# Moving the sample tile's gathered experts from the dense stretch into the head of a one-core encoder step

## The chip, the core and the metric

The kernel runs on one core of a Trainium2 chip. The core has TensorE (PE in the profile), VectorE (DVE), ScalarE (ACT), GpSimd (POOL) and SyncE (SP), each with its own instruction queue that is worked off in order, and 16 DMA engines that all queues share. The metric is the device time of one execution in microseconds; the time before is the median of three runs.

## The reference

The step is one layer of a streaming encoder on 1024 prompt frames and 64 sample frames. After the mixers (windowed attention and retention) every frame `h` goes through PEER: 8 heads pick 16 experts each out of 16384 by product keys, so 128 experts for a frame, and

```python
s1, i1 = lax.top_k(s[:, :, 0], PEER_TOPK)
s2, i2 = lax.top_k(s[:, :, 1], PEER_TOPK)
...
eidx = jnp.take_along_axis(cand_i, sel, axis=-1)
g = jax.nn.softmax(top_s, axis=-1)
act = jax.nn.gelu(jnp.einsum('tpkd,td->tpk', u_tab[eidx], xb, preferred_element_type=jnp.float32))
w = (g * act).astype(xb.dtype)
return jnp.einsum('tpk,tpkd->td', w, v_tab[eidx])
```

followed by `layer_norm(ALPHA * h + peer, ln2_g, ln2_b)`. Rows of `u_tab` and `v_tab` have 1024 float32 values.

## The kernel before

**Tiles.** There are nine tiles of frames: eight of the prompt (0 to 7, 128 frames each) and `TS` = 8, the 64 sample frames. Tiles 0 to 4 (`DENSE`) are computed against all 16384 experts on PE, with a table `G` of gate weights in DRAM. Tiles 8, 5, 6 and 7 (`GT`, in this order) are *gathered*: for each of a frame's 128 experts, rows of `u` and `v` are fetched. A *slot* is one such fetch for 128 partitions: an indirect DMA on POOL's queue (line 239) brings 128 rows of 8 KB (u and v side by side, 1.05 MB) into a buffer `uv`. The sample tile has two experts of its 64 frames side by side in a slot, so 64 slots; the other three have 128 each: 448 in all.

**Stages.** `head` does the groups `[8, 0, 1]`, `[2, 3]`, `[4, 5]`, `[6, 7]` in turn: `qkv`, `mixer`, `posts`, `keys`. After a group's keys its tiles are appended to `bg`, generators of `route` that find the expert indices on DVE. `mid` builds `G` for tiles 2, 3 and 4 with one-hot products. The *dense stretch* runs 128 passes of `u_mm` (48 matmuls into `pA` each) with the `v_mm` products into `y` between them.

**G by scatter.** For tiles 0 and 1 (`SCAT`) the table `G` is filled by 256 scatters on POOL's queue (line 373), 128 for each tile; from the 17th on a tile's scatter adds to what is there, and each waits on POOL until the tile's one before has landed. `scatter` is called in `bulk`, in the keys and in `mid`.

**The order by hand.** The program's order is written by a planner that adds up estimated times (`Est`). In the head, `bulk` keeps a credit `cr` of DVE time (0.92 of PE's estimated time less what DVE was given, at most 7) and spends it on steps of `bg`. For POOL it keeps `pq`, the time to which POOL is booked: a scatter adds `SCC` = 1.6 and a gather `GTC` = 1.1, and a scatter is placed only while `pq` is no more than 5 ahead:

```python
if t in sc and links[t] < 128 and (n < rush or (due[t] <= now() and ctl["pq"] <= now() + 5.0)):
```

A slot may be placed once the planner's clock has reached `avail`, which is the booked time plus a `slack`:

```python
ctl["avail"][k] = max(est.t["dma"] + 2.0, max(ctl["pq"], now()) + ctl["slack"])
```

While it is built, the kernel prints how many scatters of tiles 0 and 1 stand in the program at each group's end: 0 and 0, 43 and 41, 98 and 97, 128 and 128.

**A slot before.** All 448 slots are in the dense stretch (`ctl["uvp"]` is `None` until then). `slot` multiplies and sums u with `h` on DVE (`uv<-uv,ph`, with a read of the accumulator), `settle` does the gelu and the gate on ACT (`gav`), `accum` adds the weighted v row to `pacc` in PSUM on DVE. At most `LEAD` = 3 gathers are ahead, in `NB` = 4 buffers. After a tile's last slot, `finish` and `norm_out` do the last norm, whose power is on POOL (`mvf`); `norm_out` lets four steps go by between it and the DVE instruction that reads it.

Of the kernel before, what the change touches and what calls it, by code (L numbers as in the profile page):

```python
# [9 lines left out]
F32 = mybir.dt.float32  # L10
# [4 lines left out]
AF = mybir.ActivationFunctionType  # L15
OP = mybir.AluOpType
AX = mybir.AxisListType

D = 1024
# [5 lines left out]
TS = NTP  # L25
# [12 lines left out]
NB, LEAD = 4, 3  # L38
# [15 lines left out]
SL = (30.0, 5, 5.0)  # L54
FA, FB = 8, 5
NVS, NWB = 6, 6
KW = 256 + NM + 1
KWS = 128 + NS + NM + 1

# [76 lines left out]
def hymba_peer_step(ctx, tc, a, o):  # L136
    nc0 = tc.nc
    est = Est()
# [7 lines left out]
    nc = NC  # L146
    ctx.enter_context(tc.manual_schedule())
    gat = ctx.enter_context(tc.tile_pool(name="gat", bufs=1))
    rx = ExitStack()
    rt = rx.enter_context(tc.tile_pool(name="rt", bufs=1, side="right"))  # L150
# [7 lines left out]
    sfac = gat.tile([128, 1], F32, name="sfac")  # L158
# [6 lines left out]
    spill = {}  # L165
# [43 lines left out]
    ready = {t: False for t in range(NTP + 1)}  # L209
    GT = [t for g in GROUPS for t in g if t not in DENSE]  # L210
    slots = [(t, j) for t in GT for j in range(64 if t == TS else 128)]
    ctl = dict(most=3, k=0, issued=0, done=-1, avail=[0.0] * len(slots), fin=[], uvp=None, ln2=None, gps=None, lead=LEAD, slack=9.0, cr=0.0, pe0=0.0, dve0=0.0, ph=0, pq=0.0)
    tl, rows_uv = {}, {}

    def open_tile(t):
        d = spill[t]
        h1 = gat.tile([128, D], F32, name="gh1")
        g = gat.tile([128, 128], F32, name="gg", bufs=2)
        idx = gat.tile([128, 128], I32, name="gi", bufs=2)
        if t == TS:  # L220
            for i, (lo, hi) in enumerate(((0, NS), (NS, 128))):
                nc.sync.dma_start(h1[lo:hi], d["h1"])
                nc.sync.dma_start(g[lo:hi, 0:64], d["g"][:, i * 64:(i + 1) * 64])
                nc.sync.dma_start(idx[lo:hi, 0:64], d["idx"][:, i * 64:(i + 1) * 64])
        else:
            nc.sync.dma_start(idx, d["idx"])
            nc.sync.dma_start(h1, d["h1"])
            nc.sync.dma_start(g, d["g"])
        av = gat.tile([128, 128], F32, name="gav", bufs=2)
        tl[t] = dict(h1=h1, g=g, idx=idx, av=av, left=64 if t == TS else 128)  # L230

    def issue():
        k = ctl["issued"]
# [37 lines left out]
    def finish(t, d):  # L271
        r, q = d["acc"], 128
        ln2, late = ctl["ln2"], t == TS
        if ln2 is None or t == TS:
            x = ctl["uvp"].tile([128, 2 * D], F32, name="lnx", tag="uv")
            ln2 = [x[:, 0:D], x[:, D:2 * D]]
            nc.sync.dma_start(ln2[0], rows_bcast(a["ln2_g"], D))
            if t == TS:
                q = NS
                nc.sync.dma_start(ln2[1][0:NS], r[NS:128])  # L280
                yield
                yield
                yield
                yield
                nc.vector.tensor_tensor(r[0:NS], r[0:NS], ln2[1][0:NS], op=OP.add)
            nc.sync.dma_start(ln2[1], rows_bcast(a["ln2_b"], D))
        yield from norm_out(gat, t, r, q, ln2)

    def norm_out(pool, t, r, q, ln2, st=None):
        wide = st is not None  # L290
        if not wide:
            st = pool.tile([128, 2, 6], F32, name="stf", bufs=2)
            for i, x in enumerate(halves(r)):
                nc.vector.bn_stats(st[:q, i], x[:q])
        mv = pool.tile([128, 3], F32, name="mvf", bufs=2)
        nc.vector.bn_aggr(mv[:q, 0:2], st[:q])
        nc.vector.tensor_scalar(mv[:q, 1:2], mv[:q, 1:2], EPS, None, op0=OP.add)
        nc.gpsimd.tensor_tensor(mv[:q, 2:3], mv[:q, 1:2], epsc[:q, 0:1], op=OP.pow)
        if wide:
            nc.gpsimd.tensor_tensor(mv[:q, 0:1], mv[:q, 0:1], mv[:q, 2:3], op=OP.mult)  # L300
            nc.gpsimd.tensor_scalar(mv[:q, 0:1], mv[:q, 0:1], -1.0, None, op0=OP.mult)
            yield
            nc.scalar.activation(r[:q], r[:q], AF.Identity, bias=mv[:q, 0:1], scale=mv[:q, 2:3])
            yield
            nc.gpsimd.tensor_tensor(r[:q], r[:q], ln2[0][:q], op=OP.mult)
            yield
            eng = nc.gpsimd if DENSE.index(t) in PAD else nc.vector
            eng.tensor_tensor(r[:q], r[:q], ln2[1][:q], op=OP.add)
            nc.sync.dma_start(o["y_p"][t * 128:(t + 1) * 128, :], r)
            return  # L310
        for _ in range(4):
            yield
        nc.vector.scalar_tensor_tensor(r[:q], r[:q], mv[:q, 0:1], ln2[0][:q], op0=OP.subtract, op1=OP.mult)
        yield
        nc.vector.scalar_tensor_tensor(r[:q], r[:q], mv[:q, 2:3], ln2[1][:q], op0=OP.mult, op1=OP.add)
        if t == TS:
            nc.sync.dma_start(o["y_s"], r[:q])
        else:
            nc.sync.dma_start(o["y_p"][t * 128:(t + 1) * 128, :], r)
# [5 lines left out]
    def prefetch():  # L325
        if ctl["uvp"] is None:
            return
        while (ctl["issued"] < len(slots) and ctl["issued"] < ctl["k"] + ctl["lead"]
               and ready[slots[ctl["issued"]][0]]):
            issue()  # L330

# [29 lines left out]
    def now():  # L361
        return max(est.t["pe"], est.t["dve"])

    links, due = {t: 0 for t in SCAT}, {t: 0.0 for t in SCAT}
    sc = {}

# [14 lines left out]
        return n  # L381

    zq = [(t, i) for t in SCAT for i in range(8)]
    zeros = rt.tile([128, 512], F32, name="zeros")
    nc.vector.memset(zeros, 0.0)

    def clear():
        t, i = zq.pop(0)
        nc.sync.dma_start(spill[t]["G"].rearrange("(p a n) o -> p a (n o)", p=128, n=512)[:, i * 4:(i + 1) * 4],
                          zeros[:, None, :].to_broadcast([128, 4, 512]))  # L390

    def pump(most, room=1.0):
        prefetch()
# [17 lines left out]
    def log(what):  # L411
        print("phase end", what, {k: round(v) for k, v in est.t.items()}, ctl["k"], len(bg), list(links.values()))
# [13 lines left out]
    def bulk(n):  # L426
        pe, dve = est.t["pe"], est.t["dve"]
        ctl["cr"] = min(CRMAX, ctl["cr"] + CRATE * (pe - ctl["pe0"]) - (dve - ctl["dve0"]))
        ctl["n"] = ctl.get("n", 0) + 1
        if zq and ctl["n"] % ZP == 0:  # L430
            clear()
        while scatter():
            pass
        for i in range(n):
            if ctl["cr"] <= 0.0:
                break
            d0 = est.t["dve"]
            step_bg()
            ctl["cr"] -= est.t["dve"] - d0
        ctl["pe0"], ctl["dve0"] = est.t["pe"], est.t["dve"]  # L440

    def head(hx):
# [2 lines left out]
        wrk = hx.enter_context(tc.tile_pool(name="wrk", bufs=2))  # L445
        sml = hx.enter_context(tc.tile_pool(name="sml", bufs=2))
        late = hx.enter_context(tc.tile_pool(name="late", bufs=4))
        pps = [hx.enter_context(tc.tile_pool(name=f"pps{i}", bufs=1, space=bass.MemoryType.PSUM)) for i in range(2)]

        def bank(tag):  # L450
# [549 lines left out]
        for gi, tiles in enumerate(GROUPS):  # L1000
# [33 lines left out]
            for t in sorted(tiles, key=lambda t: t not in DENSE):  # L1034
                bg.append(route(t, VI[t], NS if t == TS else 128))
                kind.append(t in DENSE)
            log("group")

    def route(t, VI, q):
        V, I = VI[:, 0], VI[:, 1].bitcast(U32)  # L1040
# [565 lines left out]
```

## Time and profile before

| | |
|---|---|
| median of 3 runs | 3328.54 us (3322.7 to 3331.77) |
| the profiled execution | 3355.53 us, span 3353.8 us |
| PE busy | 2904.7 us, 87% |
| DVE busy | 2265.5 us, 68% |
| POOL busy | 1781.7 us, 53% |
| ACT busy | 1115.8 us, 33% |
| granted PE clock, mean | 0.934 |
| DMA | 813.19 MB, 242 GB/s over the span |

Times in the rows are microseconds from the span's start, or nanoseconds where a row says mean ns. A row that names a releaser says what ended the engine's idle time. A busy share is an average over its stretch. The head takes the first 1030 us or so, the dense stretch begins at about 1260 us.

### The profile page before, as it was taken

To read this page: it belongs to the slowest core of one execution; us is meant where nothing else is said; L and a number is where in the kernel's file an instruction comes from. 1 tells how busy PE (TensorE), PEld (TensorE's weight loads), DVE (VectorE), ACT (ScalarE), POOL (GpSimd) and SP (SyncE) were. 2 spreads that over 40 slices of the span, in tenths; PEclk is the share of its full clock that TensorE was granted. 3 is DMA by queue.
4 is the path that set the end of the run, shared out by engine and by line. 5 is a ranking of instruction groups with operands and counts; after the bars stand their busy time and mean duration, and the time that the engine had idled before them with its cause. 6 is when DMAs were issued, how large, how long until landed. Compare 5 with 4: busy or idle time off the path is not lost.

```text
span 3353.8 us, 43782 instructions
## 1 busy us (share of the span) xinstructions
PE 2904.7 (87%) x15212; PEld 2495.5 (74%) x15212; DVE 2265.5 (68%) x5539; ACT 1115.8 (33%) x2599; POOL 1781.7 (53%) x1326
## 2 busy tenths in 40 slices
PE   4999889898996568888899988989899899989996
PEld 3777767677775557777788877878788788878895
DVE  1436976738639964776777777777778677877424
ACT  2332232332424663333333333333333333333221
POOL 0000155676663555665666666666666566666544
PEclk8999899899897789999999999999999999999998
DMA  6435235436432468898999989899989899999531
GB/s 178 145 112 213 82 84 145 95 62 167 97 79 79 114 181 325 326 346 304 349 355 354 350 336 340 321 347 341 355 323 361 318 349 349 351 367 340 199 98 63
DMA packets 296470, 813.19 MB, mean 242 GB/s; under 512 B 58296, under 2 KB 164520, under 8 KB 229176
## 3 DMA queue, kind: packets, MB, share of 16 engines
q0 software_dynamic: 97792, 469.94, 39.3%
q1 hardware_dynamic: 198024, 340.12, 29.9%
q8 instruction: 120, 1.97, 0.2%
q14 instruction: 102, 0.84, 0.1%
q10 hardware_dynamic: 432, 0.33, 0.0%
HBM read 753.04 MB, written 56.97 MB: 242 GB/s over the span
## 4 chain that ended last, share of the span: by engine, by line
PE 39%; DVE 22%; DMA 13%; issue 11%; POOL 10%; ACT 3%; SPq 1%; POOLq 0%; DVEq 0%; ACTq 0%
PE pA L108 13%; PE y L108 10%; DMA uv<-uv,gi 9%; PE pv L108 4%; PE pq L108 4%; DVE VI L108 4%; PE pa L108 3%; POOL uv L239 3%; POOL vl L108 3%; DVE pacc L108 3%; DVE ge L108 2%; DVE ob L108 2%; POOL ul L108 2%; POOL wl L108 2%; DVE oh L108 2%
## 5 line engine op out<-in xcount | busy, mean ns | idle before, releaser
L239 POOL DMA_INDIRECT uv<-uv,gi x448 | 432.1, 965 | 619.8 <-DVE pacc L108 561.2
L373 POOL DMA_INDIRECT G<-sg,si x256 | 382.3, 1493 | 620.2 <-DVE si L108 383.3
L108 DVE SCALAR_TENSOR_TENSOR uv<-uv,ph 128x1024 f32<-128x1024 f32 x448 | 544.1, 1215 | 238.1 <-DMA uv<-uv,gi 234.0
L108 PE MATMUL y<-vh,wh 128*128 128x512 f32 x1280 | 530.7, 415 | 185.1 <-DVE Y L108 182.9
L108 DVE SCALAR_TENSOR_TENSOR pacc<-uv,gav,pacc 128x1024 f32<-128x1024 f32 x448 | 575.6, 1285 | 2.2 <-ACT pacc L108 2.1
L108 PE MATMUL y<-vl,wh 128*128 128x512 f32 x1280 | 521.7, 408 | 2.0 <-POOL vl L108 2.0
L108 PE MATMUL y<-vh,wl 128*128 128x512 f32 x1280 | 520.8, 407 | 0.0
L108 PEld LDWEIGHTS y<-vh,wh 128*128 128x128 f32 x1280 | 250.8, 196 | 270.8 <-DVE Y L108 173.6
L108 DVE TENSOR_TENSOR Y<-y,Y 128x512 f32<-128x512 f32 x420 | 280.6, 685 | 178.8 <-PE y L108 175.1
L108 POOL TENSOR_TENSOR vl<-vr,vh 128x512 fp32r<-128x512 f32 x256 | 327.9, 1294 | 100.5 <-ACT vh L108 49.9
L108 PEld LDWEIGHTS pA<-xhi,uh 128*128 128x128 f32 x2048 | 331.5, 199 | 37.1 <-DVE ge L108 24.1
L108 PE MATMUL pA<-xhi,uh 128*128 128x320 f32 x2048 | 338.6, 320 | 23.3 <-DVE ge L108 23.3
L108 ACT ACTIVATE gav<-gav 128x1 f32<-128x1 f32 x448 | 88.7, 198 | 706.5 <-DVE uv L108 693.7
L108 PE MATMUL pA<-xlo,uh 128*128 128x320 f32 x2048 | 321.7, 309 | 0.0
L108 PE MATMUL pA<-xhi,ul 128*128 128x320 f32 x2048 | 321.2, 309 | 0.0
L108 POOL TENSOR_TENSOR ul<-ur,uh 128x1024 fp32r<-128x1024 f32 x128 | 309.6, 2418 | 4.8 <-ACT uh L108 2.5
L108 PEld LDWEIGHTS pA<-xlo,uh 128*128 128x128 f32 x2048 | 306.5, 188 | 0.0
L108 PEld LDWEIGHTS pA<-xhi,ul 128*128 128x128 f32 x2048 | 305.6, 187 | 0.0
L108 PEld LDWEIGHTS y<-vh,wl 128*128 128x128 f32 x1280 | 252.9, 198 | 57.0
L108 PEld LDWEIGHTS y<-vl,wh 128*128 128x128 f32 x1280 | 252.5, 197 | 48.9 <-POOL vl L108 2.9
L108 ACT ACTIVATE pA<-pA 128x640 f32<-128x640 f32 x128 | 88.0, 688 | 511.9 <-PE pA L108 505.9
L108 DVE TENSOR_TENSOR ge<-pA,gt 128x640 f32<-128x640 f32 x128 | 105.2, 822 | 212.0 <-ACT pA L108 145.3
(287 smaller groups left out, 4385.4 us busy)
## 6 DMA issues: line engine op xcount, KB each, us to landing
ur<-ut SPq DMA_DIRECT2D x128, 512.0 KB
vr<-vt SPq DMA_DIRECT2D x256, 256.0 KB
gt<-G SPq DMA_DIRECT2D x320, 128.0 KB
w<-w_r SPq DMA_DIRECT2D x32, 1024.0 KB
G<-gs SPq DMA_DIRECT2D x24, 1024.0 KB
G<-zeros SPq DMA_DIRECT2D x16, 1024.0 KB
w<-w_out SPq DMA_DIRECT2D x16, 1024.0 KB
w<-w_pq SPq DMA_DIRECT2D x16, 1024.0 KB
```

The costliest lines, as they stand in the source:

```text
L108: return f(*a, **k)
L239: nc0.gpsimd.indirect_dma_start(out=R, out_offset=None, in_=a["uv"], in_offset=bass.IndirectOffsetOnAxis(ap=tl[t]["idx"][:, j:j + 1], axis=0))
L373: nc0.gpsimd.indirect_dma_start(out=spill[t]["G"], out_offset=bass.IndirectOffsetOnAxis(ap=idx[:, j:j + 1], axis=0), in_=g[:, j:j + 1], in ...
```

## The change

The 64 slots of the sample tile are placed in the head, as credit allows, once that tile is routed; slots that find no place there go on in the dense stretch. In `bulk`, each step of `bg` is followed by a `half` if credit is left: either the u product of the next slot (`udot_head`) or the v product of an earlier one (`vacc_head`). Both are on DVE in SBUF; the gelu is five ACT instructions on one column in place of the two of `settle`. Up to `LEADH` = 4 gathers are ahead, in `NBH` = 5 buffers of a pool of the head, and `slack` is 12. To make room, the tile of zeros with which `G` is cleared is halved. At the head's end the slots in flight are worked off. `finish` and `norm_out` let fewer steps go by, for all gathered tiles.

```diff
-    ctl = dict(most=3, ..., lead=LEAD, slack=9.0, ...)
+    ctl = dict(most=3, ..., lead=LEADH, head=True, turn=0, slack=12.0, ...)
...
+        gh = None
+        if ctl["head"]:
+            gh = rt.tile([128, 64], F32, name="ggh")
+            nc.scalar.activation(gh, g[:, 0:64], AF.Copy, scale=0.5)
...
-                yield
-                yield
                 nc.vector.tensor_tensor(r[0:NS], r[0:NS], ln2[1][0:NS], op=OP.add)
...
-        for _ in range(4):
-            yield
+        yield
         nc.vector.scalar_tensor_tensor(r[:q], r[:q], mv[:q, 0:1], ln2[0][:q], op0=OP.subtract, op1=OP.mult)
...
-        while (ctl["issued"] < len(slots) and ctl["issued"] < ctl["k"] + ctl["lead"]
+        while (ctl["issued"] < (64 if ctl["head"] else len(slots)) and ctl["issued"] < ctl["k"] + ctl["lead"]
...
+    def udot_head(k):
+        t, j = slots[k]
+        d = tl[t]
+        R = rows_uv[k]
+        av = d["av"][:, j:j + 1]
+        if j == 0:
+            d["acc"] = gat.tile([128, D], F32, name="gacc")
+            nc.scalar.activation(d["acc"], d["h1"], AF.Copy, scale=sfac)
+        nc.vector.scalar_tensor_tensor(R[:, 0:D], R[:, 0:D], 1.0, d["h1"], op0=OP.mult, op1=OP.mult, accum_out=av)
+        u = rt.tile([128, 3], F32, name="gu", bufs=4)
+        nc.scalar.activation(u[:, 0:1], av, AF.Square, scale=math.sqrt(0.044715))
+        nc.scalar.activation(u[:, 1:2], u[:, 0:1], AF.Identity, scale=av, bias=av)
+        nc.scalar.activation(u[:, 2:3], av, AF.Copy, scale=d["gh"][:, j:j + 1])
+        nc.scalar.activation(u[:, 0:1], u[:, 1:2], AF.Tanh, scale=math.sqrt(2.0 / math.pi))
+        nc.scalar.activation(av, u[:, 0:1], AF.Identity, scale=u[:, 2:3], bias=u[:, 2:3])
+
+    def vacc_head(k):
+        t, j = slots[k]
+        d = tl[t]
+        nc.vector.scalar_tensor_tensor(d["acc"], rows_uv.pop(k)[:, D:2 * D], d["av"][:, j:j + 1], d["acc"],
+                                       op0=OP.mult, op1=OP.add)
...
+    def half():
+        prefetch()
+        k = ctl["k"]
+        can = k < ctl["issued"] and ctl["avail"][k] <= now()
+        if ctl["done"] < k - 1 and (ctl["turn"] or not can):
+            ctl["turn"] = 0
+            vacc_head(ctl["done"] + 1)
+        elif can and ctl["done"] >= k - 2:
+            ctl["turn"] = int(ctl["done"] < k - 1)
+            udot_head(k)
+            ctl["k"] = k + 1
...
-    zeros = rt.tile([128, 512], F32, name="zeros")
+    zeros = rt.tile([128, 256], F32, name="zeros")
...
             step_bg()
             ctl["cr"] -= est.t["dve"] - d0
+            if ctl["cr"] <= 0.0:
+                break
+            d0 = est.t["dve"]
+            half()
+            ctl["cr"] -= est.t["dve"] - d0
...
+        ctl["uvp"] = hx.enter_context(tc.tile_pool(name="uvh", bufs=NBH))
...
+        ctl["lead"] = 0
+        while ctl["k"] < ctl["issued"] or ctl["done"] < ctl["k"] - 1 or ctl["fin"]:
+            est.t["pe"] += 0.5
+            half()
+        ctl["head"], ctl["uvp"] = False, None
```

## Rows read from the trace of the kernel before

**Rows 1.** Dense stretch: busy us (count) of PE, PEld, DVE, ACT, POOL; PEclk, DMA share, GB/s.

```profile
1300.00:3100.00 1800.00, 1618.25 (x8585) 1438.75 (x8585) 1358.05 (x1803) 585.90 (x1432) 1134.21 (x880) 0.95 0.92 342
3160.00:3288.00 128.00, 128.00 (x718) 116.70 (x717) 29.43 (x41) 30.43 (x45) 60.12 (x38) 1.00 0.28 89
```

**Rows 2.** The same two stretches, PE's matmuls into pA alone; PEclk, DMA share, GB/s.

```profile
1300.00:3100.00 1800.00, 807.08 (x5282) 0.95 0.92 342
3160.00:3288.00 128.00, 64.83 (x432) 1.00 0.28 89
```

**Rows 3.** The first of them, POOL's gathers alone.

```profile
1300.00:3100.00 1800.00, 421.37 (x437) 0.95 0.92 342
```

**Rows 4.** Waits of PE, dense stretch with gathers: us in total, times, longest.

```profile
PE y L108 <- DVE Y L108: 177.5, 85, 8.7
```

**Rows 5.** Groups of instructions over the whole span: shapes, count, busy, mean ns, idle.

```profile
L108 DVE SCALAR_TENSOR_TENSOR pacc<-uv,gav,pacc 128x1024 f32<-128x1024 f32 x448 | 575.6, 1285 | 2.2 <-ACT pacc L108 2.1
L108 DVE SCALAR_TENSOR_TENSOR uv<-uv,ph 128x1024 f32<-128x1024 f32 x448 | 544.1, 1215 | 238.1 <-DMA uv<-uv,gi 234.0 <-issue 3.1
...
L239 POOL DMA_INDIRECT uv<-uv,gi x448 | 432.1, 965 | 619.8 <-DVE pacc L108 561.2 <-issue 24.3 <-DMA gt<-G 11.9
...
L108 ACT ACTIVATE gav<-gav,gg 128x1 f32<-128x1 f32 x448 | 132.1, 295 | 14.5
...
L108 ACT ACTIVATE gav<-gav 128x1 f32<-128x1 f32 x448 | 88.7, 198 | 706.5 <-DVE uv L108 693.7 <-issue 11.5
...
L108 DVE DVE_READ_ACCUMULATOR uv<-uv,ph 128x1 f32 x448 | 37.0, 83 | 0.0
```

**Rows 6.** Timeline, the end of the sample tile's routing.

```profile
477.77 0.49 SPq L85 DMA_DIRECT2D idx<-idx  x1
```

**Rows 7.** Busy time by stretch, the head from there on (columns as in Rows 1).

```profile
480.00:525.00 45.00, 42.01 (x222) 35.75 (x220) 12.75 (x55) 10.12 (x28) 30.42 (x20) 1.00 0.32 59
525.00:600.00 75.00, 62.19 (x336) 51.87 (x337) 61.35 (x389) 22.11 (x48) 35.98 (x23) 0.91 0.60 177
...
675.00:750.00 75.00, 72.63 (x375) 59.64 (x372) 26.74 (x103) 22.14 (x67) 53.14 (x35) 1.00 0.36 67
...
480.00:1002.00 522.00, 472.00 (x2401) 383.79 (x2400) 314.35 (x1590) 160.47 (x429) 335.97 (x216) 0.94 0.46 109
```

**Rows 8.** POOL's scatters alone, by stretch.

```profile
380.00:583.00 203.00, 103.84 (x78) 0.94 0.39 107
583.00:808.00 225.00, 144.93 (x93) 0.93 0.46 110
808.00:1002.00 194.00, 132.63 (x86) 0.93 0.43 92
```

**Rows 9.** Timeline of DVE where the third and fourth group begin their routes.

```profile
582.88 0.79 DVE L108 TENSOR_TENSOR cd<-VI 128x40 f32<-128x40 f32 x7
...
807.84 0.78 DVE L108 TENSOR_TENSOR cd<-VI 128x40 f32<-128x40 f32 x7
```

**Rows 10.** Waits of POOL in the head from 480 us.

```profile
POOL G L373 <- DMA G<-sg,si: 139.1, 61, 7.9
POOL G L373 <- issue: 47.4, 155, 0.5
```

**Rows 11.** Timeline of POOL, before and in a burst of weight loads.

```profile
520.45 1.55 POOL L373 DMA_INDIRECT G<-sg,si  x1 [0.30 <-issue]
522.30 1.55 POOL L373 DMA_INDIRECT G<-sg,si  x1 [0.30 <-issue]
...
545.56 1.55 POOL L373 DMA_INDIRECT G<-sg,si  x1 [7.89 <-DMA G<-sg,si]
```

**Rows 12.** Timeline of POOL, its last scatter.

```profile
1001.35 1.55 POOL L373 DMA_INDIRECT G<-sg,si  x1 [0.30 <-issue]
```

**Rows 13.** Waits of PE in the head from 480 us, the longest.

```profile
PE pt L108 <- DVE t L108: 8.8, 2, 4.5
```

**Rows 14.** POOL's groups, dense stretch with gathers.

```profile
L108 POOL TENSOR_TENSOR mvf<-mvf,epsc 128x1 f32<-128x1 f32 (+1 forms) x3 | 1.7, 568 | 8.2 <-DVE mvf L108 8.2
```

More of the change, by code (lines that the diff above doesn't have):

```diff
@@ L56 @@
 NVS, NWB = 6, 6
+NBH, LEADH = 5, 4
 KW = 256 + NM + 1
@@ L211, in hymba_peer_step @@
     slots = [(t, j) for t in GT for j in range(64 if t == TS else 128)]
-    ctl = dict(most=3, k=0, issued=0, done=-1, avail=[0.0] * len(slots), fin=[], uvp=None, ln2=None, gps=None, lead=LEAD, slack=9.0, cr=0.0, pe0=0.0, dve0=0.0, ph=0, pq=0.0)
+    ctl = dict(most=3, k=0, issued=0, done=-1, avail=[0.0] * len(slots), fin=[], uvp=None, ln2=None, gps=None, lead=LEADH, head=True, turn=0, slack=12.0, cr=0.0, pe0=0.0, dve0=0.0, ph=0, pq=0.0)
     tl, rows_uv = {}, {}
@@ L228, in open_tile @@
             nc.sync.dma_start(g, d["g"])
+        gh = None
+        if ctl["head"]:
+            gh = rt.tile([128, 64], F32, name="ggh")
+            nc.scalar.activation(gh, g[:, 0:64], AF.Copy, scale=0.5)
         av = gat.tile([128, 128], F32, name="gav", bufs=2)
-        tl[t] = dict(h1=h1, g=g, idx=idx, av=av, left=64 if t == TS else 128)
+        tl[t] = dict(h1=h1, g=g, gh=gh, idx=idx, av=av, left=64 if t == TS else 128)
     def issue():
@@ L362, in now @@
         return max(est.t["pe"], est.t["dve"])
+    def udot_head(k):
[18 more added lines that the diff above has]
+                                       op0=OP.mult, op1=OP.add)
+        ctl["done"] = k
+        d["left"] -= 1
+        if d["left"] == 0:
+            ctl["fin"].append(finish(t, d))
+    def half():
[9 more added lines that the diff above has]
+            ctl["k"] = k + 1
+        for f in list(ctl["fin"]):
+            try:
+                next(f)
+            except StopIteration:
+                ctl["fin"].remove(f)
     links, due = {t: 0 for t in SCAT}, {t: 0.0 for t in SCAT}
@@ L388, in clear @@
         t, i = zq.pop(0)
-        nc.sync.dma_start(spill[t]["G"].rearrange("(p a n) o -> p a (n o)", p=128, n=512)[:, i * 4:(i + 1) * 4],
-                          zeros[:, None, :].to_broadcast([128, 4, 512]))
+        nc.sync.dma_start(spill[t]["G"].rearrange("(p a n) o -> p a (n o)", p=128, n=256)[:, i * 8:(i + 1) * 8],
+                          zeros[:, None, :].to_broadcast([128, 8, 256]))
     def pump(most, room=1.0):
```

## The prediction

> **What bounds the kernel now.** I read the windows of the dense stretch first, because the change takes work out of it. With gathers, 1800 us hold 5282 matmuls into `pA`, so 110 passes of 48, 16.36 us each; after the last gather, 432 in 128 us are 9 passes, 14.22 us each, with PE busy all the time [rows 1, 2]. The reader is to see that the stretch has two speeds: PE sets the second, and in the first the DMA share is 0.92, against 0.28 later, and a pass takes 2.14 us more. The waits say where that shows: PE stands 177.5 us behind the sums into `Y` on DVE [rows 4], and DVE stands behind gathers that haven't landed, 234.0 us over the span [rows 5].
>
> Then I read the head from 480 us, where the sample tile's indices are written [rows 6] and its gathers could begin. PE is busy 472 of 522 us there, and DVE 314 [rows 7]; PE's longest entry in the list of waits is 8.8 us [rows 13]. PE sets the head's time, and DVE has 208 us idle. In the keys stretches, which come every 225 us (525 to 600 is one), DVE is at 61 of 75; in the mixer and posts of 675 to 750 only at 27 of 75.
>
> Last I read POOL in the head, which works for nobody there but the scatters. It shows as 64% busy, which looks like room. But its idle time is 139.1 us of waiting for a scatter's landing and 47.4 us of issue [rows 10], which with 336 busy is the whole of the 522 us: POOL always has its next scatter in hand, and never waits for the program. So I compared what POOL had begun with what the program has placed. The third group's route begins at 583 us, the fourth's at 808 [rows 9], each right behind the group's end, where the kernel prints 84 and 195 scatters placed. POOL had begun 78 at 583 us and 171 at 808 [rows 8]. It is 6 late at the first mark and 24 at the second, and at 225 / 93 = 2.42 us each that is 58 us. The last one begins at 1001 us [rows 12]. Before, this lateness costs nothing, since nobody reads `G` until the dense stretch. Gathers behind those scatters would have a reader: DVE, in the head.
>
> **The change part by part.** *Dense stretch.* 64 of 448 slots leave. The excess is 110 x 2.14 = 235 us for 437 gathers [rows 3], 0.54 us each, so 64 x 0.54 = 34.5 us. From below, PE's idle time alone is 177.5 / 437 = 0.41 us each, 26 us. There is no more to win from above: 64 slots are 16 passes' worth, and no pass goes under 14.22 us. I take -35.
>
> *`norm_out` with fewer steps.* DVE reads POOL's `mvf` sooner. POOL takes 568 ns for it and waited 8.2 us in three [rows 14]; what stands ahead on POOL now falls to DVE, at worst 8.7 us, PE's longest wait for DVE [rows 4], for each of tiles 5 to 7: 0 to 26, taken as +5, since the one step left is itself a slot.
>
> *DVE in the head.* A slot costs 1.215 + 0.083 + 1.285 = 2.58 us [rows 5], 64 of them 165 us. The 208 us idle hide it, with 42 left. Without that cover the price is 165.
>
> *ACT in the head.* Before, a slot had 198 + 295 ns; the five instructions, two like the first and three with a column operand like the second, make 1.28 us, 82 us in all, beside 160 of 522 busy [rows 5, 7]. Hidden as work. But ACT is in order: the first of the five waits for the u product, that for the gather, and behind them stand the evictions that PE needs. A late gather therefore holds DVE and ACT both.
>
> *SP and the rest.* The sample tile's six loads move from the dense stretch to 480 us, and one must wait for the write of [rows 6] to land. PE waits there for no weight, its longest entry being DVE's [rows 13]: 0, at most the 8.8 us of that row. The clearing of `G` in pieces half as long is over before any scatter: 0.
>
> *POOL in the head: the term that decides.* Between the marks the program places 111 scatters in 225 us, 2.03 us for 1.6 of the planner's units, so a unit is 1.27 us. A gather is booked at 1.1, thus 1.4 us; a slot is placed some 12 + 5 units after its gather, 21.6 us, of which the gather's own issue and bytes (0.965 us, and 1.05 MB at 342 GB/s [rows 1], 3.07 us) leave 17 us for lateness. When is the last gather placed? Four are ahead for 21.6 us, so not before 480 + 16 x 21.6 = 826 us of the time of before; not after 975, where the last keys begin, which call no `bulk`. I take 920, since near the keys little credit is left. Until then the booking has room for (440 - 64 x 1.4) / 2.03 = 172 scatters, which POOL does in 172 x 2.42 = 416 us, and 64 gathers at g each. The last is due, allowance included, by 937:
>
> 480 + 416 + 64 g - 937 = 64 g - 41 us late.
>
> No row has a gather among scatters, so g is bounded. Below, 0: 64 x 0.965 = 62 us fit into the 139 us in which POOL waits for landings anyway. With the 0.30 us of issue [rows 11] and nothing hidden it is 1.27. Above, each gather's bytes also hold the next scatter's landing: 1.27 + 3.07 = 4.34. The nearest row between is how waits go with traffic now: 139.1 us for 522 us x 109 GB/s = 57 MB, 2.4 us for each MB [rows 7, 10]; when weights come in a burst, one wait is 7.89 us, and 0.30 us with quiet queues [rows 11]. A gather is 1.05 MB, so up to 2.6 us of waits, a good half of them hidden behind POOL's own time at the next instructions: I take g = 1.27 + 0.9 = 2.2, nearer to the low end, and 100 us late. An in-order DVE hands on a steadily later queue as head time.
>
> What is late next is the mixer's chain on PE. The scatters left over run behind the last gather and end about with the head, as before.
>
> **Sum.** -35 + 5 + 100 = +70 us. The profiled execution is 3355.5 us, 27 above the runs' median of 3328.5; 3355.5 + 70 = 3425.5 there, and 3399 as a median.
>
> **The rivals.** *The head takes the slots for nothing.* POOL's waits swallow the gathers and the head keeps its length; the place is POOL's queue, the point 64 g = 41, g below 0.64 us. Then -35 + 5, 3299 us. For it speak the 139 us of waits; against it that POOL falls 58 us behind on scatters alone, where traffic is 110 GB/s, and that the gathers add 67 MB.
>
> *A little late.* g of 0.64 to 1.5 makes the last gather 0 to 55 us late, and the 42 us that DVE has left absorb part: 3320 to 3354, 3330 at the middle.
>
> *Each gather holds the stream for its bytes.* g = 4.34, 237 us late, +207: 3536 us. For it speaks the burst in [rows 11], in which a scatter waits out other queues' bytes; against it that two tiles' scatters alternate, so that one scatter lies between a landing and its waiter. The Trainium skill, "DMA: Bandwidth & Descriptors", section "Queues, rings and completion order", says the semaphore's write lands only after every earlier write of that DMA engine, across its queues. By that rule the scatter behind a gather is told as landed only when the gather's bytes are in, which is this rival; the burst's 7.89 us agrees in kind, and no run here has shown it for a gather.
>
> *The change does only part of what it says*: credit runs out and slots stay for the dense stretch. Loss and gain shrink alike; half the slots would make it about 1.27 x 32 - 41, not late, and -17: 3316. That is counted with the first rival.
>
> **How the numbers follow.** The forecast, g of 1.5 to 3.3, +25 to +140, 3354 to 3469 us, gets 0.58, because POOL's lateness is read from counts and only g is argued. The head for nothing, or fewer slots: 0.19. A little late: 0.15, two thirds of it within 0.3% (10 us, about what a measurement of this kernel can tell from no change). Bytes in full: 0.08. Faster 0.19, same 0.10, slower 0.71. The range 3305 to 3475 leaves out the last rival and the lower edge of the first.
>
> **What would show it.** Right: in the head DVE waits for `uv` from gathers, growing towards its end; POOL's gaps before scatters become longer; the head ends near 1130 us in place of 1030; the dense stretch is some 35 us shorter, with 384 gathers. Wrong: the head within 20 us of before with DVE's waits for `uv` small (g was under 1), or POOL waiting for the program, so that scatters and gathers are paced by the planner and not the other way round; or the loss in the keys, where DVE has the least room, which would be DVE's 165 us uncovered and not POOL's queue.

## The result and the profile after

The changed kernel takes 3433.64 us (median of 4 runs, 3424.46 to 3440.53), the kernel before beside it 3330.15 (4 runs, 3322.7 to 3333.78): 1.0312 times, interval 1.0281 to 1.0343, so 103 us slower. The forecast was 3399 us, with a range of 3305 to 3475.

The first question is where the 103 us lie. The boundaries of the stages can be read from groups of instructions by tile: the last key search (`FIND_INDEX8`) ends the head, the first matmul into `pG` begins `mid`, the first into `pA` the dense stretch (in the kernel before that is at 1235 us, not at about 1260). A row gives min/median/max ns, then the first and last start. The kernel before:

```profile
L108 DVE FIND_INDEX8 VI<-VI,tmp x144: 275/285/297, 292.4 to 1029.0; 128x8 uint32<-128x128 f32 x128, 64x8 uint32<-64x128 f32 x16
...
L108 PE MATMUL pG<-oh x768: 274/275/582, 1031.4 to 1235.4; 128*128 128x128 f32 x192
...
L108 PE MATMUL pA<-xhi,uh x2048: 303/308/634, 1235.4 to 3291.5; 128*128 128x320 f32 x187
```

And the changed kernel, with the slots and scatters of its head:

```profile
L109 DVE FIND_INDEX8 VI<-VI,tmp x144: 272/289/311, 293.2 to 1167.7; 128x8 uint32<-128x128 f32 x128, 64x8 uint32<-64x128 f32 x16
...
L109 PE MATMUL pG<-oh x768: 274/276/582, 1184.1 to 1388.3; 128*128 128x128 f32 x192
...
L109 PE MATMUL pA<-xhi,uh x2048: 303/308/633, 1388.4 to 3370.9; 128*128 128x320 f32 x187
...
L418 POOL DMA_INDIRECT G<-sg,si x256: 954/1557/2638, 384.1 to 1142.2; - x128
...
L244 POOL DMA_INDIRECT uv<-uv,gi x55: 933/995/1986, 486.4 to 1134.1; - x55
L109 DVE SCALAR_TENSOR_TENSOR uv<-uv,gh x55: 1205/1219/1244, 496.2 to 1174.0; 128x1024 f32<-128x1024 f32 x55
```

The reader is to see four things. The last key search comes 139 us later (1029.0 to 1167.7) and the first `pG` matmul 153 us (1031.4 to 1184.1); `mid` keeps its 204 us. POOL's last scatter, 1001 us in [rows 12], comes at 1142, and its last gather of the head at 1134, beside it. Only 55 of the 64 slots lie in the head. And the dense stretch, from the first `pA` to the span's end of 3433.0, takes 2044.6 us, where it took 2118.3.

The windows of the changed kernel (columns as in [rows 1]; the second pair counts `pA` matmuls alone, the last line POOL's gathers):

```profile
480.00:1150.00 670.00, 510.98 (x2440) 412.77 (x2439) 442.90 (x1807) 223.52 (x690) 427.34 (x276) 0.85 0.59 172
...
705.00:780.00 75.00, 44.33 (x186) 32.64 (x185) 44.88 (x131) 24.84 (x77) 54.22 (x34) 0.79 0.54 139
...
1450.00:2990.00 1540.00, 704.47 (x4647) 0.97 0.94 350
3040.00:3366.00 326.00, 165.68 (x1104) 1.00 0.31 97
...
1450.00:2990.00 1540.00, 366.96 (x381) 0.97 0.94 350
```

The first line answers to the last of [rows 7]. PE was idle 50 of 522 us there; now 159 of 670. Its own work also became slower: 2401 matmuls in 472.0 us are 197 ns each, 2440 in 511.0 are 209 ns, at a mean granted clock of 0.85 in place of 0.94. In the mixer's stretch of 705 to 780 PE works 44 of 75 us at 0.79; before, in 675 to 750, it worked 73 of 75 at 1.00 [rows 7].

The longest single wait of PE in the head before (480 to 1002 us; total, times, longest):

```profile
PE pq L108 <- ACT hmA L108: 6.6, 1, 6.6
```

And what POOL, DVE and PE waited for in the head of the changed kernel, from 480 to 1150 us:

```profile
POOL G L418 <- DMA G<-sg,si: 166.6, 67, 11.1
DVE uv L109 <- DMA uv<-uv,gi: 85.0, 17, 14.4
...
PE pt L109 <- ACT TT L109: 30.5, 9, 7.5
...
PE pm L109 <- ACT hmB L109: 24.1, 2, 20.5
```

DVE now stands 85 us behind gathers that haven't landed, in 17 waits of up to 14.4 us, and PE's single waits, at most 6.6 us before, reach 20.5 us behind evictions on ACT (its copies out of PSUM). POOL's waits for scatters, 139.1 us in the 522 us of [rows 10], are 166.6 in these 670. The chain of waits says the same with shares. Between 480 us and the first `pG` matmul the chain that ended last ran, before, through these lines:

```profile
by line: PE pv L108 16.0%; DVE VI L108 16.0%; PE pq L108 14.4%; PE pa L108 10.9%; DVE tmp L108 5.4%; PE pm L108 5.4%; DVE prd L108 4.3%; DVE ge L108 3.4%; PE po L108 3.2%; DVE Tp L108 2.7%; PE pt L108 2.3%; issue 1.7%; DVE nwt L108 1.5%; PE
```

and in the changed kernel through these:

```profile
by line: DVE VI L109 11.5%; DMA uv<-uv,gi 11.0%; DMA G<-sg,si 10.0%; POOL G L418 10.0%; issue 7.4%; DVE uv L109 4.3%; DVE gacc L109 4.2%; DVE tmp L109 3.9%; DVE prd L109 3.2%; POOL uv L244 2.7%; PE pa L109 2.7%; DVE ge L109 2.3%; DVE t L109
```

PE's matmuls led before, and POOL's queue isn't among the shares that the row shows. Now gathers, scatters and their landings hold 11.0 + 10.0 + 10.0 + 2.7 = 33.7% of 704 us, 237 us.

### The profile page after: what moved, and what is told of

Read it like the earlier page. It is cut to its first block, busy times and chain, and to the rows that moved or that the text cites. A ratio compares the mean times of both kernels' runs of the same rounds, so it can differ in the third digit from the quotient of the medians.

```text
span 3433.0 us, 43914 instructions
## 1 busy us (share of the span) xinstructions
PE 2905.2 (85%) x15212; PEld 2496.2 (73%) x15212; DVE 2274.3 (66%) x5539; ACT 1155.4 (34%) x2766; POOL 1810.6 (53%) x1326
## 4 chain that ended last, share of the span: by engine, by line
PE 34%; DVE 25%; DMA 17%; POOL 10%; issue 9%; ACT 3%; SPq 1%; POOLq 0%; DVEq 0%; ACTq 0%
PE pA L109 15%; PE y L109 12%; DMA uv<-uv,gi 9%; DVE VI L109 4%; POOL uv L244 3%; DVE pacc L109 3%; POOL vl L109 2%; PE pq L109 2%; DMA G<-sg,si 2%; POOL G L418 2%; DMA vr<-vt 2%; DVE ge L109 2%; DVE ob L109 2%; PE pa L109 2%; PE pv L109 2%
## 5 line engine op out<-in xcount | busy, mean ns | idle before, releaser
L418 POOL DMA_INDIRECT G<-sg,si x256 | 408.4, 1595 | 645.3 <-DVE si L109 383.7
L109 PE MATMUL y<-vh,wh 128*128 128x512 f32 x1280 | 522.8, 408 | 140.6 <-DVE Y L109 140.6
L109 DVE SCALAR_TENSOR_TENSOR uv<-uv,ph 128x1024 f32<-128x1024 f32 x393 | 477.5, 1215 | 192.0 <-DMA uv<-uv,gi 189.9
L109 PE MATMUL y<-vh,wl 128*128 128x512 f32 x1280 | 513.3, 401 | 0.0
L109 DVE SCALAR_TENSOR_TENSOR pacc<-uv,gav,pacc 128x1024 f32<-128x1024 f32 x393 | 504.9, 1285 | 0.4 <-ACT pacc L109 0.4
L109 POOL TENSOR_TENSOR vl<-vr,vh 128x512 fp32r<-128x512 f32 x256 | 328.2, 1296 | 166.6 <-ACT vh L109 111.5
L109 PEld LDWEIGHTS pA<-xhi,uh 128*128 128x128 f32 x2048 | 322.5, 194 | 36.3 <-DVE ge L109 25.1
L109 ACT ACTIVATE gav<-gav 128x1 f32<-128x1 f32 x393 | 77.7, 198 | 593.3 <-DVE uv L109 592.6
```

What stands on the lines that cost most here:

```text
L109: return f(*a, **k)
L418: nc0.gpsimd.indirect_dma_start(out=spill[t]["G"], out_offset=bass.IndirectOffsetOnAxis(ap=idx[:, j:j + 1], axis=0), in_=g[:, j:j + 1], in ...
```

## The experiments

Two theories stood against each other. **The queue**: POOL does 256 scatters and the gathers in one stream; the gathers come late, and DVE, which works in order, makes their lateness the head's. **The slots' own work**: their DVE and ACT instructions lie in the way of what PE waits for. The first nine kernels take these apart, the last three the other terms of the sum. A time without a range is that of a single run; two profiles of the kernel before differ by 8 us at the last key search (1029.0 and 1021.2), so a few us at one place say nothing.

### Slots without gathers

```diff
+        if ctl["head"]:
+            if k < NBH:
+                res.append(ctl["uvp"].tile([128, 2 * D], F32, name=f"uvr{k}", bufs=1))
+                nc0.vector.memset(res[k], 0.0)
+            R = res[k % NBH]
...
-        nc0.gpsimd.indirect_dma_start(out=R, out_offset=None, in_=a["uv"],
+        if not ctl["head"]:
+            nc0.gpsimd.indirect_dma_start(out=R, out_offset=None, in_=a["uv"],
```

> The changed kernel with the 55 slots that the planner places in the head working on buffers that are already there (zeros): the same DVE and ACT instructions at the same places of the program, without the 55 gathers, so the sample tile's result is left incomplete. Theory A (slots wait for gathers that come late through POOL's queue): the loss in the head goes; the last key search, at 1168 us in the changed kernel and 1029 before, ends at 1030 to 1065, and the whole takes 3310 to 3345 us. Theory B (the slots' own work, 55 x 2.58 = 142 us of DVE and the ACT steps that stand in front of PE's evictions, is not covered): the last key search stays at 1140 to 1170 and the whole at 3410 to 3440.

3365.24 us. The head's slots read zeros that stand there from the start, so `y` of the sample tile lacks them; all their DVE and ACT work is done.

```profile
L109 DVE FIND_INDEX8 VI<-VI,tmp x144: 272/278/292, 292.3 to 1089.9; 128x8 uint32<-128x128 f32 x128, 64x8 uint32<-64x128 f32 x16
...
L427 POOL DMA_INDIRECT G<-sg,si x256: 952/1554/2593, 383.3 to 1011.9; - x128
```

The own work alone makes the head 61 us longer (1029.0 to 1089.9), with POOL's last scatter only 11 us later. The prediction had it hidden; here it is not.

### Without gathers and without the small ACT steps

```diff
-        nc.scalar.activation(u[:, 0:1], av, AF.Square, scale=math.sqrt(0.044715))
-        nc.scalar.activation(u[:, 1:2], u[:, 0:1], AF.Identity, scale=av, bias=av)
-        nc.scalar.activation(u[:, 2:3], av, AF.Copy, scale=d["gh"][:, j:j + 1])
-        nc.scalar.activation(u[:, 0:1], u[:, 1:2], AF.Tanh, scale=math.sqrt(2.0 / math.pi))
-        nc.scalar.activation(av, u[:, 0:1], AF.Identity, scale=u[:, 2:3], bias=u[:, 2:3])
```

> The changed kernel without the head's gathers, and without the five ScalarE instructions of a slot there as well: the two VectorE products are left, so y of the sample tile is another. Without the gathers alone the last key search began at 1089.9 us, 61 us later than before. Theory A (the 61 us are ScalarE's: its small steps stand ahead of the evictions that PE waits for): the last key search starts at 1030 to 1045, and PE's waits behind ScalarE in the head shrink. Theory B (they are VectorE's, whose 165 us the idle time does not take where it lies): 1075 to 1090, about as without the gathers. Theory C, half each: near 1060.

3315.35 us.

```profile
L109 DVE FIND_INDEX8 VI<-VI,tmp x144: 273/286/298, 292.9 to 1054.4; 128x8 uint32<-128x128 f32 x128, 64x8 uint32<-64x128 f32 x16
```

Of the 61 us, 35.5 are ACT's five small steps (1089.9 to 1054.4) and 25 the two DVE products. Theory C, half each, was nearest.

### Gathers without scatters

```diff
-                nc0.gpsimd.indirect_dma_start(
-                    out=spill[t]["G"], out_offset=bass.IndirectOffsetOnAxis(ap=idx[:, j:j + 1], axis=0),
-                    in_=g[:, j:j + 1], in_offset=None, ...)
```

> The changed kernel without the 256 scatters into G (left out altogether, so tiles 0 and 1 get no expert sum), the planner's booking of them kept, so that gathers, slots and everything else stand at the same places of the program. Theory A: gathers go out at once, land within 12 us or so, and the last key search ends at 1035 to 1070 us. Theory B: 1140 to 1170, as in the changed kernel. If it is between, the gathers' traffic or their flight has a part of its own.

3366.39 us. The table `G` of tiles 0 and 1 stays empty here; slots and gathers are whole.

```profile
L109 DVE FIND_INDEX8 VI<-VI,tmp x144: 272/283/292, 291.9 to 1099.7; 128x8 uint32<-128x128 f32 x128, 64x8 uint32<-64x128 f32 x16
```

DVE's waits for gathers from 480 to 1150 us:

```profile
DVE uv L109 <- DMA uv<-uv,gi: 0.2, 1, 0.2
```

With POOL's queue to themselves the gathers are in time: DVE waits 0.2 us for them in place of 85.0, and the head is 10 us longer than without gathers (1089.9 to 1099.7), little more than two profiles of one kernel differ by. Of the changed kernel's 139 us, the scatters in the same queue are needed for 68 (1167.7 less 1099.7). But even this kernel is slower than before by 38 us, and its `G` is not even filled.

### Gathers that nobody in the head reads

```diff
-        nc.vector.scalar_tensor_tensor(R[:, 0:D], R[:, 0:D], 1.0, d["h1"], ..., accum_out=av)
-        u = rt.tile([128, 3], F32, name="gu", bufs=4)
...
+        est.t["dve"] += (66 + D) / 960.0
...
-        nc.vector.scalar_tensor_tensor(d["acc"], rows_uv.pop(k)[:, D:2 * D], ...)
+        est.t["dve"] += (66 + D) / 960.0 + 0.06
+        rows_uv.pop(k)
```

> The changed kernel with the 55 gathers issued in the head but the slots' DVE and ACT work there left out (those slots' experts are missing from the sample tile's result). POOL then runs free, as before. Theory A: the head costs nothing, last key search at 1029 to 1040 us; POOL's last scatter, at 1001 us before, comes as late as 55 gathers make it: at 1001 + 55 g - (what fits into waits), which gives g directly; 1001 means g = 0, 1071 g = 1.27, 1122 g = 2.2, 1240 g = 4.34. Theory B expects the same of the head, and says nothing of POOL.

3382.46 us. The head's 55 gathers are issued at the same places of the program, their slots' work is left out, so the sample tile's `y` lacks them.

```profile
L109 DVE FIND_INDEX8 VI<-VI,tmp x144: 272/279/292, 293.0 to 1005.6; 128x8 uint32<-128x128 f32 x128, 64x8 uint32<-64x128 f32 x16
...
L409 POOL DMA_INDIRECT G<-sg,si x256: 952/1554/1991, 384.2 to 1131.4; - x128
...
L109 PE MATMUL pG<-oh x768: 274/275/582, 1134.1 to 1335.7; 128*128 128x128 f32 x192
...
1097.06 0.99 POOL L244 DMA_INDIRECT uv<-uv,gi  x1 [0.30 <-issue]
```

And PE's longest wait from 1000 to 1340 us of this kernel:

```profile
PE pG L109 <- POOL oh L109: 140.5, 6, 132.6
```

This prices a gather in POOL's stream: (1131.4 - 1001.4) / 55 = 2.36 us. The head's other engines are done at 1006 us, and then PE stands 132.6 us in one wait, behind a one-hot product that POOL does only after its backlog. So the backlog has a reader even where no slot reads it, namely `mid`, whose products stand in the same queue: 103 us at the first `pG` (1031.4 to 1134.1).

The last row of the first fence is the fiftieth gather. In the changed kernel it goes out 5 us later, and DVE waits for it 14.40 us, just before the last keys:

```profile
1102.19 0.99 POOL L244 DMA_INDIRECT uv<-uv,gi  x1 [0.30 <-issue]
...
1114.86 1.23 DVE L109 SCALAR_TENSOR_TENSOR uv<-uv,gh 128x1024 f32<-128x1024 f32 x1 [14.40 <-DMA uv<-uv,gi]
```

So POOL alone, with nobody reading, brings this gather to within 5 us of where the changed kernel has it. That is the most direct evidence that POOL's stream, and not the slots' work, sets the place of the last slots.

One thing more: the last key search is 16 to 23 us earlier here than in the two profiles of before, and with short rows (next) it begins at 997.5. In both kernels the planner still books the slots' time, so the rest of the head stands in another order than before; whether that is what makes it faster no run shows. Against these two, the slots' own work of the first experiment costs 84 to 92 us and not 61.

### The same with short rows

```diff
-        nc0.gpsimd.indirect_dma_start(out=R, out_offset=None, in_=a["uv"],
+        src = a["uv"].rearrange("n (c k) -> (n c) k", k=64) if small else a["uv"]
+        nc0.gpsimd.indirect_dma_start(out=R[:, 0:64] if small else R, out_offset=None, in_=src,
```

> The version in which the head issues its 55 gathers and nothing there reads them, with each gather of 128 rows cut from 2048 to 64 columns, 1.05 MB to 33 KB; the sample tile's slots of the head are left out of y. With full rows POOL's last scatter began at 1131 us against 1001 before, 2.37 us for each gather. Theory A (a gather costs POOL its issue and little else): the last scatter stays near 1001 + 55 x 1.27 = 1071 or later with full rows' 1131 at most; if issue is all of it, 1120 to 1131. Theory B (bytes make the scatters behind wait, and the gather's own time hides in POOL's waits): 1001 to 1030. In between, 1050 to 1080: issue 1.27 us each and the rest bytes, as the prediction put it together.

3308.76 us.

```profile
L411 POOL DMA_INDIRECT G<-sg,si x256: 952/1554/2064, 384.7 to 1059.1; - x128
```

On POOL's timeline behind the first four gathers, the second scatter:

```profile
495.04 0.97 POOL L411 DMA_INDIRECT G<-sg,si  x1 [2.15 <-DMA G<-sg,si]
```

The gather's price falls to (1059.1 - 1001.4) / 55 = 1.05 us. So the 2.36 us are 1.05 for its place in the queue and 1.31 for its bytes. (Some of the 1.05 is no price of a gather: POOL stands 14.67 us, once, until the indices of the first gather have landed, at most 0.27 us for each of 55.) The timeline shows where the bytes bite: the second scatter behind four short gathers waits 2.15 us. In the changed kernel the one at the same place waits 10.55:

```profile
486.39 0.98 POOL L244 DMA_INDIRECT uv<-uv,gi  x1 [14.67 <-DMA gi<-idx]
...
490.19 0.93 POOL L244 DMA_INDIRECT uv<-uv,gi  x1 [0.30 <-issue]
491.42 1.00 POOL L418 DMA_INDIRECT G<-sg,si  x1 [0.30 <-issue]
502.97 1.61 POOL L418 DMA_INDIRECT G<-sg,si  x1 [10.55 <-DMA G<-sg,si]
```

The Trainium skill's rule that the prediction named as a rival ("DMA: Bandwidth & Descriptors", "Queues, rings and completion order", there of DMAs issued from SP and ACT: a semaphore's write lands only after the earlier writes of that DMA engine) agrees with this in kind. No run here tells it from a scatter whose own bytes stand behind the gathers'. The rival's full price, 3.07 us of bytes a gather, does not show: 1.31 do.

### More slack for the planner

```diff
-    ctl = dict(..., slack=12.0, ...)
+    ctl = dict(..., slack=40.0, ...)
```

> The changed kernel with slack 40 in place of 12: slots stand later behind their gathers, by 28 units of some 1.27 us; the planner then finds room for 35 slots in the head, not 55. Theory A: gathers are no longer late, DVE's waits for them in the head fall from 85 us to under 20, the last key search ends at 1030 to 1070 us, the dense stretch gains 35 x 0.44 to 0.54 = 15 to 19 us, and the whole lands at 3310 to 3355. Theory B: the loss goes with the number of slots, 35/55 of 139 us = 88 us, and the whole lands at 3395 to 3405.

3395.79 us (4 runs, 3395.48 to 3401.77), 1.0204 times the kernel before (1.0186 to 1.0223).

```profile
L109 DVE FIND_INDEX8 VI<-VI,tmp x144: 272/280/291, 292.2 to 1112.8; 128x8 uint32<-128x128 f32 x128, 64x8 uint32<-64x128 f32 x16
...
L418 POOL DMA_INDIRECT G<-sg,si x256: 953/1555/2623, 383.6 to 1086.5; - x128
...
L109 PE MATMUL pA<-xhi,uh x2048: 303/308/633, 1338.2 to 3331.9; 128*128 128x320 f32 x187
```

35 slots are left in the head, and POOL's last scatter follows them: 1001.4 + 35 x 2.43. A slack shifts a slot by a fixed time; a stream that falls further behind with each gather catches up with any of them: DVE still waits 47.2 us for gathers, where Theory A asked for under 20. The loss, 84 us at the last key search, went down with the number of slots (35/55 of 139 are 88), not with the slack. As the slots' own work shrinks with their number too, this run alone doesn't tell the two theories of this section apart.

### No slots in the keys

```diff
-            if ctl["cr"] <= 0.0:
-                break
+            if ctl["cr"] <= 0.0 or not slots_too:
+                continue
...
-                    bulk(BK[4])
+                    bulk(BK[4], False)
```

> The changed kernel, but in the keys stretches no slot is placed, only in the mixer and posts; nothing is left out of the computation. If VectorE's load in the keys is what costs (each keys stretch grew from 37 to 40 us to 37 to 58), the keys are back at 37 to 41 us each and the last key search starts 15 to 20 us earlier, at about 1150. If POOL's stream sets the end, its last scatter moves with the gathers alone: with 53 slots 1001 + 53 x 2.4 = 1128, and the last key search starts at 1150 to 1165 whatever the keys do.

3431.58 us.

```profile
L109 DVE FIND_INDEX8 VI<-VI,tmp x144: 273/284/294, 292.3 to 1173.3; 128x8 uint32<-128x128 f32 x128, 64x8 uint32<-64x128 f32 x16
...
L418 POOL DMA_INDIRECT G<-sg,si x256: 956/1558/2623, 383.2 to 1135.7; - x128
...
DVE uv L109 <- DMA uv<-uv,gi: 129.2, 20, 27.5
```

With 53 slots, all in the mixer and posts, the keys of the second group take 40 us again (58 in the changed kernel), and nothing is won: the last key search is as late as ever, behind a scatter at 1136. What was saved in the keys was waited for elsewhere: the last row shows DVE's waits for gathers (480 to 1200 us), 129.2 us where they were 85.0. In the kernels whose gathers run to the head's end, the last key search stands 25 to 38 us behind POOL's last scatter (25.5 in the changed kernel, 26.3 with the larger slack, 37.6 here, 31.8 in the next). That distance alone proves nothing, since it is 27.6 before, without a gather.

### One ACT step for a slot

```diff
+        nc.vector.scalar_tensor_tensor(u[:, 0:1], av, 0.044715, av, op0=OP.mult, op1=OP.mult)
+        nc.vector.scalar_tensor_tensor(u[:, 1:2], u[:, 0:1], 1.0, av, op0=OP.add, op1=OP.mult)
+        nc.scalar.activation(u[:, 2:3], u[:, 1:2], AF.Tanh, scale=math.sqrt(2.0 / math.pi))
...
+        nc.vector.scalar_tensor_tensor(u[:, 0:1], u[:, 2:3], 1.0, d["gh"][:, j:j + 1], op0=OP.add, op1=OP.mult)
+        nc.vector.tensor_tensor(av, u[:, 0:1], av, op=OP.mult)
```

> The changed kernel with the head's gelu written in another way: one ScalarE instruction for a slot (tanh) in place of five, and four instructions of one column more on VectorE; nothing is left out, 53 slots lie in the head. Without gathers the five ScalarE instructions cost 35 us of head. Theory A (the losses add: ScalarE's steps and the late gathers each cost their own): the last key search starts 20 to 35 us earlier than the changed kernel's 1167.7, at 1133 to 1148, and the time is 3398 to 3413. Theory B (POOL's stream is a floor; its last scatter comes at 1001 + 53 x 2.37 = 1127 whatever ScalarE does): the last key search stays at 1150 to 1168 and the time at 3416 to 3433.

3434.31 us (4 runs, 3428.67 to 3439.81), 1.0325 times before (1.0297 to 1.0354): the same as the changed kernel.

```profile
L109 DVE FIND_INDEX8 VI<-VI,tmp x144: 272/278/290, 291.9 to 1169.2; 128x8 uint32<-128x128 f32 x128, 64x8 uint32<-64x128 f32 x16
...
L419 POOL DMA_INDIRECT G<-sg,si x256: 953/1559/2584, 383.3 to 1137.4; - x128
```

DVE's waits for gathers from 480 to 1200 us:

```profile
DVE uv L109 <- DMA uv<-uv,gi: 106.9, 19, 12.7
```

The time is Theory B's, or 1 us beyond its bounds: ACT has less to do, and DVE waits longer for gathers, 106.9 us where it was 85.0. It is weaker evidence than it was meant to be. The four instructions on DVE came out at 0.16 us each, 0.63 us a slot and 33 us in all, so that part of what ACT gave back may have gone there.

### Sixteen slots

As the last kernel, with one edit more:

```diff
-        while (ctl["issued"] < (64 if ctl["head"] else len(slots)) ...
+        while (ctl["issued"] < (16 if ctl["head"] else len(slots)) ...
```

> As the version with one ScalarE step for a slot, with the head held to 16 slots, all placed by the middle of the third group; nothing is left out. Theory A (a slot costs the head about what it gives to the dense stretch): POOL's last scatter near 1001 + 16 x 2.37 = 1039, the head 10 to 20 us longer, the dense stretch 9 to 14 us shorter by the slots, and 13 us from the side edits: 3312 to 3325, no better than the 3315.7 of the side edits alone. Theory B (POOL is only 6 us late at 583 us, so the first 16 slots are free): the head no longer than before and 3300 to 3308.

3331.67 us (12 runs, 3324.05 to 3342.9), 1.0021 times before (1.0004 to 1.0038).

```profile
L109 DVE FIND_INDEX8 VI<-VI,tmp x144: 272/280/290, 294.9 to 1062.3; 128x8 uint32<-128x128 f32 x128, 64x8 uint32<-64x128 f32 x16
...
L419 POOL DMA_INDIRECT G<-sg,si x256: 954/1553/2579, 385.9 to 1048.6; - x128
...
L109 PE MATMUL pA<-xhi,uh x2048: 304/308/635, 1269.2 to 3260.0; 128*128 128x320 f32 x187
...
DVE uv L109 <- DMA uv<-uv,gi: 18.4, 3, 10.3
```

Both theories of this run asked too little of it. Sixteen slots, all issued by 668 us, make the head 33 us longer than in the first profile of before (41 in the second), 2 us a slot and more. DVE waits only 18.4 us for gathers (480 to 1200 us), so here most of it is the slots' own work and not the queue. Against the side edits alone (next) they lose 16 to 19 us. A slot in the head costs more than it gives even where POOL is hardly behind.

The other side is just as far off: with a span of 3322.3 the dense stretch takes 2053.1 us, 31 to 42 less than in the two kernels with the side edits, where 9 to 14 were expected.

### The side edits alone

The kernel before with both side edits (shorter pauses of the norm's program, smaller zeros), and with the pauses alone:

```diff
-        for _ in range(4):
-            yield
+        yield
         nc.vector.scalar_tensor_tensor(r[:q], r[:q], mv[:q, 0:1], ln2[0][:q], ...)
...
-    zeros = rt.tile([128, 512], F32, name="zeros")
+    zeros = rt.tile([128, 256], F32, name="zeros")
```

> The kernel before with the two side edits of the change alone: the shorter pauses of the norm's program, and the zeros of 256 columns cleared in pieces half as long; no slot is done in the head. The prediction's step for these two: +5 us (0 to 26) and 0, thus 3329 to 3335 us beside 3329 of before. Rival: the side edits are themselves worth part of the gain of about 50 us that the dense stretch showed where the prediction took 30 for 55 slots; then -10 us or more, 3319 or less, and a dense stretch shorter by that much with 448 gathers still in it.

> The kernel before with the shorter pauses of the norm's program alone; the zeros stay at 512 columns. The two side edits together gave 3315.7 us, ratio 0.9957. Theory A: the pauses did it, so 3312 to 3319 here. Theory B: the smaller pieces of the clearing did it, so 3326 to 3332 here.

Both: 3315.7 us (12 runs, 3304.85 to 3325.84), 0.9957 times before (0.9942 to 0.9973). Pauses alone: 3312.2 us (12 runs, 3304.34 to 3324.75), 0.9959 (0.994 to 0.9978). So the pauses give 13 us and the zeros nothing. These are the versions that beat both kernels. Where the 13 us lie is not settled: in single profiles the dense stretch of these two took 2084.1 and 2095.1 us, and of the kernel before, profiled again, 2088.5.

### The kernel before once more

> The kernel before once more, unchanged, for a second profile. Its first profile's own time was 27 us above the median of its runs, and its dense stretch 2118 us. If that time is the dense stretch's, it measures about 2090 here with a last key search at 1029 again; then 55 slots less are worth about 45 us rather than 74, and 0.8 us each against 0.54. If the head varies, the last key search moves and the dense stretch stays at 2118.

3318.3 us.

```profile
L108 DVE FIND_INDEX8 VI<-VI,tmp x144: 273/284/301, 291.8 to 1021.2; 128x8 uint32<-128x128 f32 x128, 64x8 uint32<-64x128 f32 x16
...
L108 PE MATMUL pA<-xhi,uh x2048: 304/308/633, 1228.0 to 3254.2; 128*128 128x320 f32 x187
```

With a span of 3316.5 the dense stretch is 2088.5 us, 30 less than in the first profile, and the head 8 less. The first profile of before, at 3355.5 us, lies above all its timed runs, most of it in the dense stretch. Differences of a few us between single profiles say nothing, and the gain of the dense stretch has to be counted against this profile too.

## Why the prediction came out as it did

The sign, the cause and the range were right; the time was 35 us too low.

**The price of a gather (g = 2.2) was right.** Measured: 2.36 us, 1.05 for its place in the queue and 1.31 of bytes, where 1.27 and 0.9 were put together; the two errors partly cancel. The estimate from waits per MB of traffic [rows 7, 10] held for a kind of transfer that the trace of before didn't contain at that place. In the 1.05 lies a term that was put at 0: the loads that move to 480 us keep not PE but POOL waiting, 14.67 us, with the scatters behind it.

**The place of the last gather was the step that failed.** "I take 920, since near the keys little credit is left", with 975 as the other end. The last gather of the head ran at 1134 us, 8 us before the last scatter: gathers went on to the end of the last posts, which is the 975 end of the bracket, and nearly all the scatters stood before them. With 55 gathers, and due by 975 + 17 = 992, the same sum gives 1131.4 - 992 = 139 us late, where 100 was taken for 64 gathers at 920. The last key search is 139 us late. That the two agree to the microsecond is luck; that POOL paced the head is shown by its stream, whose fiftieth gather goes out at 1097 us with no reader and at 1102 with them, and which ended at 1131 and 1142. The last slot before the last keys is the fifty-first; the other four are worked off after them. The sum's other premise, that a scatter left over costs nothing because nobody reads `G` in the head, is not the whole either: `mid` needs POOL itself, which alone would have cost 103 us. In the changed kernel it costs nothing more, since the last scatter begins 42 us before `mid`. The rest, from 139 to 153 us, lies between the last key search and `mid`, where the slots in flight are worked off; the sum had no term for it.

**DVE's and ACT's work in the head was not hidden by idle time.** 208 us of DVE idle were set against 165 us, and ACT was called hidden as work. Alone the two cost 61 us, 35 of them ACT's, whose five steps a slot measured 1.44 us (1.28 taken) and stand in order ahead of PE's evictions. An idle total covers work only where the idle time lies, and in the keys it does not [rows 7]. In the full change the work hides after all, but behind the waits for gathers, which come hardly earlier when the work is gone: at the first `pG` matmul own work alone costs 75 us, the queue alone 103, both together 153 and not 178. How the 139 us are shared can be estimated from the fiftieth gather: the own work can have cost the 5 us by which it goes out later, and the 8 us of the last two slots behind it (1114.9 to 1122.6), which leaves the queue about 126. A kernel whose slots wait for their gathers and then cost nothing was not run, so this stays an estimate. It holds for 55 slots; with sixteen, where DVE waits only 18.4 us for gathers, the own work is the larger part.

**The dense stretch gives more than was taken.** -35 for 64 slots, 0.54 us each; measured 44 us for 55 slots and the pauses, against the second profile of before, and 40 to 50 against the two kernels with the side edits. But it is no price per slot. The stretch takes 2084.1 and 2095.1 us with the side edits and no slot in the head, 2053.1 with sixteen, 2056.0 with 35 (3394.2 - 1338.2) and 2044.6 with 55. So the first sixteen go with 31 to 42 us of the gain and the other 39 with 8.5, 0.2 us each, less than the 0.54 taken. By rates, the excess of a pass is (1540 / 96.8 - 14.17) x 96.8 / 381 = 0.44 us a gather now. That -35 came near is luck; what else in the kernels with slots in the head shortens the stretch is open.

**The pauses had the wrong sign**: +5 taken, -13 measured. The bound from below was 0, from waits alone; a gain was not looked for.

**The rivals.** The head for nothing: g would have had to be under 0.64 us, and even short rows cost 1.05 (0.78 without the one wait for the indices). A little late: g of 0.64 to 1.5, excluded by 2.36. Each gather for its bytes: 4.34, no. That slots stay for the dense stretch was true of 9 of 64 and changed little. Of what would have shown the prediction wrong, a loss in the keys is there: the second group's keys take 40 us before, 58 in the changed kernel, and 47 with no gathers at all. But keeping slots out of the keys won nothing, so the keys are not what decides.

**The sum.** Against the second profile of before the first `pA` comes 160 us later, where 100 were taken, and the dense stretch is 44 us shorter, where 30 were: +116 for +70, and the two profiled runs differ by 116.5. The medians differ by 103.5; single runs of the changed kernel lie up to 9 us from its median, those of the kernel before, in later series, up to 24.

## What to carry to other kernels

An in-order queue that always has its next instruction in hand has no room, whatever its busy share says (64% here): before handing it work with a reader, count what the program has placed against what has begun, and price the new work as lateness of the whole stream. The lateness that counts is at the *last* place where the reader stands, so the end of the bracket is the safe value there, not its middle. A total of idle time is no cover either, unless it lies where the work will stand. And side edits that ride along with a change deserve a run alone: here they were the only part that made the kernel faster by itself.

## What the runs showed of the hardware

A queue of small scatters slows down for bytes that aren't its own: 55 gathers of 1.05 MB cost POOL's stream 2.36 us each, of 33 KB 1.05. And a scatter itself takes POOL longer while DVE works on slots. The scatters of the kernel with slots and no gathers, and of the one with gathers that nobody reads, from 480 to 1150 us (count, busy us, mean ns):

```profile
L427 POOL DMA_INDIRECT G<-sg,si x217 | 364.3, 1679 | 170.7 <-DMA G<-sg,si 123.4 <-issue 47.3
...
L409 POOL DMA_INDIRECT G<-sg,si x221 | 345.0, 1561 | 229.3 <-DMA G<-sg,si 183.5 <-issue 45.7
```

Before the mean is 1560 ns, in the changed kernel 1669, so it goes with DVE's slot work and not with the gathers' bytes; it makes up some 24 us of the changed kernel's POOL time.

A wait of an engine for another is paid twice at PE: where it was left idle, its mean granted clock fell from 1.00, the level of 2.4 GHz throughout, to 0.79, a part of the stretch at 1.2 GHz, in the mixer. Over the head a matmul took 209 ns in place of 197, some 31 us more for 2440 of them.
